# Second parts of the head stage's weights: made by an adding DMA instead of a vector difference

## The chip, the cores and the metric

The kernel runs on one core of a Trainium2 chip. The metric is the time of one execution on the device in microseconds (us). Three runs of the kernel before gave 1411.61, 1413.80 and 1413.81 us; the median is 1413.8 us. The profiled execution is a run of its own.

## The reference, cut to what matters

Two layers of a transformer trunk for 512 positions of width 1024, all in float32. Layer 0 mixes positions by an attention with 16 heads of 64 columns and a learned relative bias; layer 1 by a gated spatial mixing; each is followed by a squared-ReLU MLP. The change lies in layer 0's attention:

```python
q, k, v = jnp.split(h @ w_in, 3, axis=-1)
q = rms_norm(q.reshape(B, S, A_HEADS, A_HEAD_DIM), q_gain) * (A_HEAD_DIM ** -0.5)
k = rms_norm(k.reshape(B, S, A_HEADS, A_HEAD_DIM), k_gain)
...
s = jnp.einsum('bihd,bjhd->bhij', qc, kb).astype(jnp.float32) + bias
p = jax.nn.softmax(s, axis=-1).astype(vb.dtype)
return jnp.einsum('bhij,bjhd->bihd', p, vb)
...
return o @ w_out
```

`w_in` is 1024 x 3072 and `w_out` 1024 x 1024.

## The kernel before, in words

**Two parts of every operand.** TensorE multiplies in a rounded form of float32 (`float32r`). To keep the accuracy, each operand is held as a first part `hi` (the value rounded) and a second part `lo` (the value minus `hi`), and `mm3` adds up three products: hi x hi, hi x lo and lo x hi. Each weight tile is 128 x 1024 elements (512 KB). A DMA on SP's queue brings it from HBM into `raw`, ScalarE rounds it into `hi` (`A.copy`), VectorE subtracts (`V.tensor_tensor(lo, raw, hi)`), and `raw` goes back to the pool of 49 tiles (`SL`). A tile that is asked for waits until its last user is done with it.

**The stage.** Queries 0 to 11 and keys 0 to 7 are computed first. Then 16 heads run (`head_a` to `head_d`): transposes of queries and keys, a bias tile by DMA and a small memset of its corner on GpSimd, scores, softmax, transposes of the probabilities, the product with the values. In each pair of heads, GpSimd also spreads the reciprocals of the sums over a wide tile (the copy at L1210). Between the pieces of the heads, TensorE computes the rest of the projections: seven *fills* of 256 columns each (`filler`), in the order v0, v1, k2, q3, k3, v2, v3. Each fill multiplies four blocks of 128 rows by two weight tiles, here called a and b; the first multiplication of a block needs tile a's `hi`, the second its `lo`, and the thirteenth tile b. `fill_load` asks for the next fill's tiles while the one before is computed. `out_load(0)` and `out_load(1)` bring the two halves of `w_out`, four tiles each, called o0a to o0d and o1a to o1d; `out_early` multiplies the first three tiles of the first half while the last heads still run.

**What sets the order.** From the start of the heads to their end the order of instructions on every engine is set by a scheduler in the build, by its own estimate of durations; in the output projection behind them TensorE's order is the one written. On the chip each engine and each DMA queue runs its list strictly in order: whatever waits holds all that stands behind it. SP's queue issues all loads; GpSimd's (POOL's) list holds, in this stage, the sixteen memsets (L1178) and eight copies (L1210) alone.

Of the kernel before, what the change touches and what calls it, by code (L numbers as in the profile page):

```python
# [10 lines left out]
F32R = mybir.dt.float32r  # L11
I32 = mybir.dt.int32
AF = mybir.ActivationFunctionType
ALU = mybir.AluOpType
AX = mybir.AxisListType

P = 128
S = 512
D = 1024
NT = S // P  # L20
KD = D // P
# [31 lines left out]
def trunk_kernel(  # L53
# [20 lines left out]
    V, A, G, T, SP = nc.vector, nc.scalar, nc.gpsimd, nc.tensor, nc.sync  # L74
# [7 lines left out]
    SL = Slots(sp, NSLOT, "s")  # L82
    PS = Slots(pp, 8, "p")

    def f32(ap):
        return ap.bitcast(F32)
# [68 lines left out]
    def raw_tile(shape):  # L155

        t, i = SL.get(shape, F32)
        return t, lambda: SL.free(i)

    def flat(src, offset, ap):  # L160
        return bass.AP(tensor=src.tensor, offset=src.offset + offset, ap=ap)
# [217 lines left out]
    def wload(src, nk, k0=0, engs=(V,)):  # L379
        n = src.shape[1]  # L380
        kp = 1024 // n
        w, ids = [], []
        for k in range(k0, k0 + nk, kp):
            raw, done = raw_tile([P, kp, n])
            loaded[0] = SP.dma_start(raw, src[k * P:(k + kp) * P, :].rearrange("(k p) n -> p k n", p=P))
            hi, i = SL.get([P, kp, n], F32R)
            lo, j = SL.get([P, kp, n], F32R)
            A.copy(hi, raw)  # L388
            engs[len(ids) // 2 % len(engs)].tensor_tensor(lo, raw, f32(hi), ALU.subtract)  # L389
            done()  # L390
            w += [(hi[:, o, :], lo[:, o, :]) for o in range(kp)]
            ids += [i, j]
        return w, ids

    def wload_slabs(src, offset, count, n, engs=(V,)):

        w, ids = [], []
        for s in range(count):
            raw, done = raw_tile([P, 1024 // n, n])
            loaded[0] = SP.dma_start(  # L400
                raw.rearrange("p k n -> p (k n)"), flat(src, offset + s * P * 1024, [[1024, P], [1, 1024]])
            )
            hi, i = SL.get([P, 1024 // n, n], F32R)
            lo, j = SL.get([P, 1024 // n, n], F32R)
            A.copy(hi, raw)
            V.tensor_tensor(lo, raw, f32(hi), ALU.subtract)
            done()
            w += [(hi[:, o, :], lo[:, o, :]) for o in range(1024 // n)]
            ids += [i, j]
        return w, ids  # L410
# [111 lines left out]
    class Spent:  # L522
# [33 lines left out]
        def done(self, m):  # L556
            self.op.pop(m).free()
# [496 lines left out]
    for ci in range(1, 4):  # L1054
# [14 lines left out]
        k = ci * NC  # L1069
# [49 lines left out]
    with behind(), tc.issue_after(split[0].ins):  # L1119
        k_w, k_ids = wload_slabs(a_w_in, D * 768, 4, 512)  # L1120
# [167 lines left out]
    fw, fss, fps = {}, {}, [None]  # L1288

    def fill_load(n, cb):  # L1290
        if (n, cb) not in fw:
            i = {"q": -3, "k": -1, "v": 3}[n] + cb
            with tc.issue_after(split[0].ins), tc.issue_after(q_done.ins):
                fw[n, cb] = wload_slabs(a_w_in, D * (1280 + i * 256), 2, 256)

    def filler(count):
        for _ in range(count):
# [4 lines left out]
            if t == 0:  # L1302
                fill_load(n, cb)
                if (n, hf) not in qk:
                    qk_new(n, hf)
            if t == 2 and len(fill) > 2:
                fill_load(*fill[2][:2])
# [37 lines left out]
    out_w, out_ids, out_ps = {}, {}, {}  # L1345

    def out_load(hf):
        out_w[hf], out_ids[hf] = wload(a_w_out[0][:, hf * 512:hf * 512 + 512], KD)

    def out_early(t, n=6):  # L1350
        out_ps[t] = bank()
# [2 lines left out]
    for hd in range(H + 1):  # L1354
        if hd + 2 < H:
            head_a(hd + 2)
        filler(2 if hd < 10 else 1)
        bg(2 if hd < 8 else 1 if hd < 12 else 0)
        if hd + 1 < H:
            head_b(hd + 1)  # L1360
        if hd == 12:
            out_load(0)
        if H - 3 <= hd < H:
            out_early(hd - H + 3)
        if hd < H:
            head_c(hd)
        if hd > 0:
            head_d(hd - 1)
# [6 lines left out]
    in_order()  # L1375
    load_x()
    out_load(1)
    out_early(NT - 1)
    oTs = split_of(oT["t"])
# [102 lines left out]
    for hf in range(2):  # L1482
        raw, done = raw_tile([P, 4, P])
# [6 lines left out]
        a, i = SL.get([P, 2, 512], F32R)  # L1490
# [157 lines left out]
```

## Time and profile before

| what | value |
|---|---|
| median of three runs | 1413.8 us |
| profiled execution | 1417.19 us |
| its span, first to last instruction | 1415.2 us |
| TensorE busy, share of the span | 98% |
| VectorE busy, share of the span | 72% |
| ScalarE busy, share of the span | 50% |
| head stage | about 88 to 284 us of the span |

The profiled execution's span is 1.4 us above the median, so a difference that is worked out on the span is put onto the median. In the windows of the trace the columns are the length, the busy time of each engine (with its instructions), the granted clock of TensorE (1.00 is full speed), the busy share of the sixteen DMA engines and what they moved. In timelines a row has its start, its length, the engine and line, the operation, and in brackets how long the engine had stood idle before it and what ended that. "SPq" is the issue of a DMA on SP's queue; the load lands some microseconds later.

### The profile page before, as it was taken

Reading aid. Unit: us, or ns where it says so; the run is one execution under the profiler, and the core shown is the slowest. Engines: PE = TensorE matmul, PEld = TensorE weight load, DVE = VectorE, ACT = ScalarE, POOL = GpSimd, SP = SyncE. Lnnn points to the kernel's source line nnn. Section 1 sums busy time; section 2 is a strip of 40 time slices with the busy share of each in tenths; the row PEclk is TensorE's granted clock in tenths of the full one; section 3 lists DMA queues with packets and bytes.
Section 4 is the critical chain, followed back from the end, with each engine's and each line's share of the span. In section 5 each row is a group of like instructions: output and inputs, shape, how many; then the busy total and the mean of one; then the engine's idle time right before and its main releaser. Section 6 shows DMA issues by size and latency. Waiting matters only on the chain.

```text
span 1415.2 us, 18899 instructions
## 1 busy us (share of the span) xinstructions
PE 1390.1 (98%) x7226; PEld 1190.7 (84%) x7226; DVE 1021.7 (72%) x1494; ACT 710.7 (50%) x1229; POOL 9.5 (1%) x34
## 2 busy tenths in 40 slices
PE   9999988999999999999999998999999999999998
PEld 8899987789888888888888887888889988888887
DVE  6889998676668878777986745567577376866883
ACT  5537667555454544646677343134345355453630
POOL 0000000000000000000000000000000000000000
PEclk8999999999999999999999999999999999999999
DMA  9656566573253361456223344335437225242151
GB/s 371 241 141 212 168 182 189 177 278 106 77 193 120 121 221 60 147 181 223 82 82 120 134 134 141 96 106 186 131 114 276 75 79 189 60 149 89 30 164 60
DMA packets 82171, 208.94 MB, mean 148 GB/s; under 512 B 7576, under 2 KB 8992, under 8 KB 82080
## 3 DMA queue, kind: packets, MB, share of 16 engines
q1 hardware_dynamic: 82080, 207.72, 44.8%
q8 instruction: 57, 0.93, 0.3%
q14 instruction: 34, 0.28, 0.1%
HBM read 190.92 MB, written 8.39 MB: 141 GB/s over the span
## 4 chain that ended last, share of the span: by engine, by line
PE 88%; DMA 5%; DVE 3%; ACT 2%; SPq 1%; issue 1%; DVEq 0%; ACTq 0%
PE p L92 85%; DMA s<-in_a_w_in 2%; DMA s<-in_ada_w 1%; PE p L1546 1%; DMA s<-in_a_w_out 1%; PE p L1238 1%; PE p L315 1%; DMA s<-in_b_w_in 1%; SPq L1163 0%; DVE s L389 0%; ACT s L1205 0%; DVE s L955 0%; DMA s<-in_ffn_w 0%; DVE s L1200 0%; DVE s L1154 0%
## 5 line engine op out<-in xcount | busy, mean ns | idle before, releaser
L92 PE MATMUL p<-s,s 128*128 128x512 f32 (+2 forms) x6568 | 1325.6, 362 | 9.8 <-ACT s L388 2.8
L92 PEld LDWEIGHTS p<-s,s 128*128 128x128 f32 x6568 | 1112.8, 190 | 195.3 <-ACT s L388 3.2
L484 DVE TENSOR_TENSOR s<-s,s 128x1024 fp32r<-128x1024 f32 x234 | 280.2, 1220 | 108.0 <-PE p L92 52.8
L483 ACT CAST s<-s 128x1024 fp32r<-128x1024 f32 x234 | 241.7, 1051 | 173.7 <-PE p L92 108.2
L389 DVE TENSOR_TENSOR s<-s,s 128x1024 fp32r<-128x1024 f32 x80 | 96.4, 1219 | 59.0 <-ACT s L388 52.8
L388 ACT CAST s<-s 128x1024 fp32r<-128x1024 f32 x80 | 83.6, 1052 | 81.1 <-DMA s<-in_b_w_in 30.6
L631 DVE TENSOR_TENSOR s<-s,s 128x1024 f32<-128x1024 f32 x64 | 77.3, 1220 | 36.2 <-DMA s<-in_ffn_w 32.9
L739 ACT ACTIVATE r<-p 128x512 f32<-128x512 f32 x64 | 38.1, 595 | 114.8 <-PE p L92 114.8
L194 DVE SCALAR_TENSOR_TENSOR s<-s,cs,s 128x1024 f32<-128x1024 f32 x70 | 89.6, 1280 | 8.1 <-DMA s<-in_ada_w 7.3
L517 DVE TENSOR_TENSOR s<-p,s 128x512 f32<-128x512 f32 x104 | 70.4, 684 | 33.9 <-PE p L92 32.6
L745 ACT ACTIVATE s<-r 128x256 f32<-128x256 f32 (+1 forms) x112 | 44.9, 443 | 1.2
L424 DVE TENSOR_TENSOR tr<-p,s 128x512 f32<-128x512 f32 (+1 forms) x33 | 21.9, 669 | 30.3 <-PE p L92 30.1
L1205 ACT ACTIVATE s<-s,nm 128x128 f32<-128x128 f32 (+3 forms) x64 | 36.0, 564 | 6.8 <-DVE nm L1200 6.5
L1527 ACT CAST s<-s 128x512 fp32r<-128x512 f32 x24 | 14.5, 620 | 43.5 <-DVE s L1525 24.9
L1552 DVE TENSOR_TENSOR s<-p,s 128x256 fp32r<-128x256 f32 x48 | 19.9, 417 | 21.7 <-ACT s L1551 21.7
L1200 DVE CUSTOM_DVE_ANT_0 s<-p,s 128x128 f32<-128x128 f32 (+3 forms) x64 | 29.6, 484 | 7.8 <-issue 4.5
L1523 ACT ACTIVATE s<-p 128x512 f32<-128x512 f32 x24 | 14.4, 598 | 40.5 <-PE p L92 40.2
L530 DVE TENSOR_TENSOR s<-s,s 128x1024 f32<-128x1024 f32 x28 | 33.5, 1218 | 1.0 <-PE p L92 0.9
L304 ACT ACTIVATE s<-s 128x512 f32<-128x512 f32 x24 | 15.3, 637 | 34.0 <-DVE s L425 34.0
L1238 PE MATMUL p<-ident,s 128*128 128x128 f32 x160 | 25.2, 277 | 7.2 <-DVE s L1267 5.8
L1243 DVE TENSOR_TENSOR s<-p,s 128x512 fp32r<-128x512 f32 (+3 forms) x64 | 29.0, 483 | 3.8 <-ACT s L1242 3.4
L1242 ACT CAST s<-p 128x512 fp32r<-128x512 f32 (+3 forms) x64 | 25.0, 429 | 12.8 <-PE p L1238 12.5
(141 smaller groups left out, 760.6 us busy)
## 6 DMA issues: line engine op xcount, KB each, us to landing
s<-in_ffn_w SPq DMA_DIRECT2D x128, 512.0 KB, 4.6
s<-in_ada_w SPq DMA_DIRECT2D x96, 512.0 KB, 4.7
s<-in_b_w_in SPq DMA_DIRECT2D x48, 512.0 KB, 5.2
s<-in_b_w_out SPq DMA_DIRECT2D x24, 512.0 KB, 4.7
s<-in_a_w_in SPq DMA_DIRECT2D x22, 512.0 KB, 5.1
s<-s SPq DMA_DIRECT2D x64, 128.0 KB, 2.7
s<-in_x SPq DMA_DIRECT2D x8, 512.0 KB, 5.7
s<-in_a_rel_bias SPq DMA_DIRECT2D x16, 256.0 KB, 2.9
```

Source lines behind the costliest of these rows:

```text
L92: T.matmul(ps, lhsT, rhs, start=start, stop=stop, skip_group_check=more)
L194: V.scalar_tensor_tensor(acc, r, ck, acc, ALU.mult, ALU.add)
L388: A.copy(hi, raw)
L389: engs[len(ids) // 2 % len(engs)].tensor_tensor(lo, raw, f32(hi), ALU.subtract)
L483: A.copy(self.hi, raw)
L484: mark[0] = V.tensor_tensor(self.lo, raw, f32(self.hi), ALU.subtract)
L517: V.tensor_tensor(dst, ps, dst, ALU.add)
L631: V.tensor_tensor(x[0], y_[0], z[0], ALU.subtract)
L739: A.activation(r, ps, AF.Relu)
L745: A.activation(d, v, AF.Square)
L1205: A.activation(pt[it], pt[it], AF.Exp, bias=nm[:, it:it + 1], scale=-1.0, accum_out=sm[:, it:it + 1])
L1238: T.transpose(ps[:, it * P:(it + 1) * P], b["pt"][it][:, jt * P:(jt + 1) * P], ident)
```

## The change

A new function `wsplit` takes the place of `wload_slabs` for the seven fills (14 tiles) and of `wload` for the output weights (8 tiles). The load into `raw` and the rounding into `hi` stay. `raw` is given back as soon as it is rounded. Then ScalarE writes the negative of `hi` into `lo`, and a DMA that GpSimd issues reads the same weights from HBM a second time and adds them into `lo`. So each of 22 tiles loses one VectorE instruction, and gains one ScalarE instruction and one DMA of 512 KB on GpSimd's queue.

```diff
+    def wsplit(srcs, n):
+
+        w, ids = [], []
+        for src in srcs:
+            hi, i = SL.get([P, 1024 // n, n], F32R)
+            lo, j = SL.get([P, 1024 // n, n], F32R)
+            raw, done = raw_tile([P, 1024 // n, n])
+            SP.dma_start(raw, src)
+            A.copy(hi, raw)
+            done()
+            A.activation(lo, f32(hi), AF.Copy, scale=-1.0)
+            G.dma_start(lo, src, accum_op=ALU.add)
+            w += [(hi[:, o, :], lo[:, o, :]) for o in range(1024 // n)]
+            ids += [i, j]
+        return w, ids
...
             with tc.issue_after(split[0].ins), tc.issue_after(q_done.ins):
-                fw[n, cb] = wload_slabs(a_w_in, D * (1280 + i * 256), 2, 256)
+                fw[n, cb] = wsplit([
+                    flat(a_w_in, D * (1280 + i * 256) + s * P * 1024, [[1024, P], [256, 4], [1, 256]])
+                    for s in range(2)
+                ], 256)
...
     def out_load(hf):
-        out_w[hf], out_ids[hf] = wload(a_w_out[0][:, hf * 512:hf * 512 + 512], KD)
+        out_w[hf], out_ids[hf] = wsplit([
+            a_w_out[0][k * 256:k * 256 + 256, hf * 512:hf * 512 + 512].rearrange("(k p) n -> p k n", p=P)
+            for k in range(4)
+        ], 512)
```

The build's scheduler sets the head stage anew; behind it, from the end of the output projection's first multiplications on, TensorE's order is row for row the same. Line numbers of the changed kernel are higher by 16 to 22 from `gemm_tok` on. Three places of the order matter below.

**GpSimd's list around fills q3 and k3.** Before, between the copy of the second pair of heads and the copy of the fourth (L1210; the memsets at L1178 are those of heads 6 to 9):

```order
L1210 COPY s_153_1511<-rs 128x512
L1178 MEMSET s_178_1746 64x64
L1178 MEMSET s_186_1879 64x64
L1210 COPY s_182_1833<-rs 128x512
L1178 MEMSET s_205_2081 64x64
L1178 MEMSET s_215_2216 64x64
L1210 COPY s_209_2168<-rs 128x512
```

Now (L1226 are the copies, L1194 the memsets, L423 the adding DMAs; in the order of the list they are those of q3a, q3b, k3b, k3a and v2a):

```order
L1226 COPY s_153_1517<-rs 128x512
L423 DMA s_161_1569<-in_a_w_in 128x1024
L1194 MEMSET s_178_1754 64x64
L423 DMA s_164_1576<-in_a_w_in 128x1024
L1194 MEMSET s_186_1887 64x64
L1226 COPY s_182_1841<-rs 128x512
L423 DMA s_191_1898<-in_a_w_in 128x1024
L1194 MEMSET s_205_2091 64x64
L423 DMA s_188_1891<-in_a_w_in 128x1024
L1194 MEMSET s_215_2226 64x64
L423 DMA s_217_2230<-in_a_w_in 128x1024
```

The second tile of q3 stands behind the memset of head 6, both tiles of k3 behind the copy of the third pair, and k3a behind the memset of head 8 as well.

**GpSimd's list around the first half of the output weights.** Now (memsets of heads 13, 14 and 15, the copy of the seventh pair, and the adding DMAs of o0c, o0b, o0a and o0d):

```order
L1194 MEMSET s_270_2811 64x64
L1194 MEMSET s_281_2949 64x64
L423 DMA s_291_3018<-in_a_w_out 128x2x512
L1194 MEMSET s_299_3075 64x64
L1226 COPY s_283_3001<-rs 128x512
L423 DMA s_288_3011<-in_a_w_out 128x2x512
L423 DMA s_285_3004<-in_a_w_out 128x2x512
L423 DMA s_294_3025<-in_a_w_out 128x2x512
L1226 COPY s_307_3213<-rs 128x512
```

Tile o0a, which TensorE needs first, stands behind the memset of head 15, the copy of the seventh pair and o0b.

**SP's list around k3.** Before (L400 are the two loads of k3, L1163 the copies of keys between tiles, L1177 the bias tiles of heads 7 and 8):

```order
L1177 DMA s_186_1879<-in_a_rel_bias 128x512
L179 DMA s_179_1803<-in_ada_w 128x1024
L400 DMA s_187_1882<-in_a_w_in 128x1024
L1163 DMA s_175_1719<-s_177_1721 64x512 x4
L1163 DMA s_176_1720<-s_177_1721 64x512 x4
L400 DMA s_190_1888<-in_a_w_in 128x1024
```

Now:

```order
L1193 DMA s_186_1887<-in_a_rel_bias 128x512
L1179 DMA s_175_1727<-s_177_1729 64x512 x4
L1179 DMA s_176_1728<-s_177_1729 64x512 x4
L179 DMA s_193_1992<-in_ada_w 128x1024
L419 DMA s_192_1899<-in_a_w_in 128x1024
L419 DMA s_189_1892<-in_a_w_in 128x1024
```

Both loads of k3 now stand behind the eight key copies; before, k3a stood ahead of them.

## The prediction

> **What bounds the kernel now.** I read the page first. TensorE is the bound:
>
> ```profile
> span 1415.2 us, 18899 instructions
> PE 1390.1 (98%) x7226; PEld 1190.7 (84%) x7226; DVE 1021.7 (72%) x1494; ACT 710.7 (50%) x1229; POOL 9.5 (1%) x34
> ```
>
> All that TensorE stands idle in the whole span is 25 us. The order of its work differs only in the head stage, so I took that stage as one window:
>
> ```profile
> 88.00:284.00 196.00, 182.01 (x1276) 167.24 (x1275) 169.28 (x393) 128.76 (x300) 7.30 (x22) 0.97 0.61 184
> ```
>
> Here TensorE (first number after the length) is idle for 196.0 - 182.0 = 14.0 us, VectorE (third) is busy for 169 of 196 us, more than anywhere else, and the clock is 0.97, worth another 0.03 x 196 = 5.9 us. So **the whole gain that can be had is about 20 us**, however much VectorE is relieved. The timeline of TensorE shows where the idle time lies:
>
> ```profile
> 136.92 1.49 PE L92 MATMUL p<-s,s 128*128 128x512 f32 x8 [0.62 <-DVE nm L1200]
> 140.14 7.31 PE L92 MATMUL p<-s,s 128*128 128x256 f32 x56 [0.83 <-DVE nm L1200]
> 161.68 0.66 PE L1149 MATMUL p<-ident,s 128*128 128x128 f32 x4 [0.52 <-DVE nm L1200]
> 162.84 7.30 PE L92 MATMUL p<-s,s 128*128 128x256 f32 x56 [0.50 <-DVE nm L1200]
> 184.68 0.47 PE L92 MATMUL p<-s,s 128*128 128x256 f32 x2 [0.78 <-DVE s L1243]
> 186.90 5.24 PE L92 MATMUL p<-s,s 128*128 128x256 f32 x21 [1.75 <-ACT s L405]
> 241.38 0.83 PE L1238 MATMUL p<-ident,s 128*128 128x128 f32 x4 [3.12 <-DVE s L1267]
> 261.13 0.33 PE L1238 MATMUL p<-ident,s 128*128 128x128 f32 x1 [2.72 <-DVE s L1267]
> 262.07 5.98 PE L92 MATMUL p<-s,s 128*128 128x512 f32 x18 [0.61 <-DVE s L1243]
> ```
>
> Two kinds: small waits under 1 us on VectorE, and three of 1.75 to 3.3 us that stand beside weight tiles that came late (fill v2 at 186.90, o0 at 241, o1 at 261). After one of the second kind the clock is low for 5 us:
>
> ```profile
> 186.90:189.40 2.50, 2.50 (x7) 2.18 (x8) 2.50 (x9) 1.65 (x6) 0.00 (x0) 0.54 0.95 183
> 189.40:192.00 2.60, 2.60 (x16) 2.45 (x15) 2.60 (x11) 1.78 (x4) 0.00 (x0) 0.78 0.95 256
> ```
>
> That costs 0.46 x 2.5 + 0.22 x 2.6 = 1.7 us on top of the wait. I charge it to each new wait of 2 us or more.
>
> **The change part by part.** What leaves and what comes has its duration in the groups of this window:
>
> ```profile
> L406 DVE TENSOR_TENSOR s<-s,s 128x1024 fp32r<-128x1024 f32 x10 | 12.2, 1222 | 5.0 <-ACT s L405 4.7
> L405 ACT CAST s<-s 128x1024 fp32r<-128x1024 f32 x10 | 10.5, 1054 | 12.5 <-DMA s<-in_a_w_in 12.5
> L389 DVE TENSOR_TENSOR s<-s,s 128x1024 fp32r<-128x1024 f32 x8 | 9.7, 1217 | 2.8 <-ACT s L388 2.8
> ```
>
> VectorE loses 18 differences in the window, 12.2 + 9.7 = 21.9 us (four more, for v0 and v1, lie before it, under a TensorE that does not wait). ScalarE gains 18 negatives; for one I take the rounding of the same tile, 1.05 us, together 19 us onto 129 of 196: it stays below VectorE's load of before, so I cost it at nothing but latency. `raw` comes free one difference earlier, 1.2 us; nothing waits for it alone.
>
> What TensorE pays with is **latency of the second part**. Before, `lo` was there 1.22 us after `hi`. Now a negative and a DMA stand there. No adding DMA is in this trace. The nearest row is a plain load of the same 512 KB, issue to landing:
>
> ```profile
> L400 SPq DMA_DIRECT2D s<-in_a_w_in x18: 327/382/1105, 32.6 to 192.5; - x18
> DMA to landing us min/median/max: 3.6/5.0/9.3
> ```
>
> From below 3.6 us, the quickest. From above 10 us, two median loads one behind the other (read what stands there, then write the sum). An adding transfer has to read another 512 KB; the engines are busy at 0.61 in this window, so the added 11.5 MB find room. I take 6.0 us, near the plain median. The Trainium skill, "DMA: Bandwidth & Descriptors", section "Anatomy of one DMA — SWDGE (gpsimd) path", gives DMAs that GpSimd issues 2.0 us plus bytes / 436e3, an estimate of 3.2 us for this tile; by it the sum below falls under zero, and no row here shows such a DMA.
>
> Now each fill. The rows are the issue of its last load, the end of preparation before, GpSimd's items that the new DMAs stand behind, and TensorE's first use (quoted above for q3 at 140.14, k3 at 162.84, v2 near 186.9):
>
> ```profile
> 104.93 1.10 SPq L400 DMA_DIRECT2D s<-in_a_w_in  x1
> 111.50 1.21 DVE L406 TENSOR_TENSOR s<-s,s 128x1024 fp32r<-128x1024 f32 x1
> 118.12 7.28 PE L92 MATMUL p<-s,s 128*128 128x256 f32 x56
> 126.79 1.08 SPq L400 DMA_DIRECT2D s<-in_a_w_in  x2
> 131.61 2.58 DVE L406 TENSOR_TENSOR s<-s,s 128x1024 fp32r<-128x1024 f32 x2 [0.46 <-ACT s L405]
> 138.50 0.14 POOL L1178 MEMSET s<- 64x64 f32 x1 [8.56 <-PE p L92]
> 147.27 0.53 SPq L400 DMA_DIRECT2D s<-in_a_w_in  x1
> 154.65 1.22 DVE L406 TENSOR_TENSOR s<-s,s 128x1024 fp32r<-128x1024 f32 x1
> 157.28 0.61 POOL L1210 COPY s<-rs 128x512 f32<-128x512 f32 x1 [15.38 <-DVE ru L150]
> 159.83 0.14 POOL L1178 MEMSET s<- 64x64 f32 x1 [1.93 <-PE p L1238]
> 181.16 0.33 SPq L400 DMA_DIRECT2D s<-in_a_w_in  x1
> 188.21 1.22 DVE L406 TENSOR_TENSOR s<-s,s 128x1024 fp32r<-128x1024 f32 x1
> ...
> 179.40 0.53 SPq L179 DMA_DIRECT2D s<-in_ada_w  x1
> 201.45 1.22 DVE L406 TENSOR_TENSOR s<-s,s 128x1024 fp32r<-128x1024 f32 x1 [1.64 <-ACT s L405]
> 209.73 5.50 PE L92 MATMUL p<-s,s 128*128 128x256 f32 x43
> ```
>
> - *k2*: ready at 112.7 before, used from 118.4. Its second tile's DMA can start near 114 (load at 105, about 5 us to land, rounding, negative among ScalarE's other work) and lands at 120; TensorE comes to tile b after 12 multiplications of 0.13 us, at 120. **+0.3**.
> - *q3*: ready at 134.2. Tile a's DMA starts near 133 and is in time. Tile b's stands behind the memset of head 6, 138.50, which itself waits for a bias tile: lands at 138.7 + 6 = 144.7. TensorE wants b at 142.5 (12 multiplications and four score ones after 140.14, 2.3 us). **+2.2**, and its clock, **+1.7**.
> - *k3*: its DMAs stand behind the copy of 157.28, and tile a's behind the memset of 159.83 too: it lands at 166 and is wanted at 162.84. That is 3.2; but TensorE comes later by q3's wait, while only part of GpSimd's list moves with it. I take half, **+1.6**.
> - *v2*: the second load came at 181.16 and was ready at 189.43. Now it stands one load and one bias tile earlier on SP's list, at 179.40; with landing, rounding and negative the DMA starts at 186 and lands at 192. That is 2.6 later than before; half for the same reason, **+1.3**. Its clock is paid already.
> - *v0, v1, v3*: ready early enough; v3 had 7 us between 202.7 and 209.7, and its last load keeps its place on SP. **0**.
>
> For the output weights:
>
> ```profile
> 233.76 1.51 SPq L385 DMA_DIRECT2D s<-in_a_w_out  x3
> 240.73 0.61 POOL L1210 COPY s<-rs 128x512 f32<-128x512 f32 x1 [4.66 <-DVE rs L1206]
> 242.61 0.14 POOL L1178 MEMSET s<- 64x64 f32 x1 [1.27 <-DMA s<-in_a_rel_bias]
> 265.99 1.21 DVE L389 TENSOR_TENSOR s<-s,s 128x1024 fp32r<-128x1024 f32 x1
> 270.86 14.49 PE L92 MATMUL p<-s,s 128*128 128x512 f32 x65
> ```
>
> TensorE began with o0 right after 241.9. Now o0a stands behind the memset of head 15, the copy of the seventh pair and o0b: not before 242.6, landing at 248.6. The new order puts some 15 other instructions ahead, 2 us, so TensorE waits from 243.9. **+4.7**; the clock fell here before as well. o1 was ready at 267.2 and used 42 multiplications of 0.22 us after 270.86, at 280: its 13 us cover the DMAs. **0**; without that cover each microsecond would count in full.
>
> Sum of the costs: 0.3 + 2.2 + 1.7 + 1.6 + 1.3 + 4.7 = 11.8 us. What comes back: of 14.0 us idle, 1.75 and 3.12 are in my terms and 3.3 stands at the end (261 and 262), which leaves 5.8 us of small waits, nearly all on VectorE; 5 of them go. At the end VectorE stood behind a difference for o1; now ScalarE stands behind the rounding and a negative; I give back half of 3.3 + 1.7, 2.5 us. 11.8 - 7.5 = +4.3; I say **+5**, span 1420, and against the median of 1413.8 **1419 us**.
>
> **The rivals.**
>
> *Faster: the DMAs land fast.* With 3.6 us, q3 is in time, k3 waits 0.4, v2 nothing, o0 2.3, and no new clock loss: 2.7 against a relief of 7.5 to 10.8 (all small waits and the whole end). That is -5 to -8, **1407**. For it: VectorE is the fullest engine after TensorE, and the small waits are its. Against: the median row is 5.0, not 3.6, and the order on GpSimd's list delays the start whatever the landing. It decides below a landing of about 4.6 us. By the fit in the Trainium skill, "DMA: Bandwidth & Descriptors" (quoted above), this would be the case.
>
> *Much slower: an adding DMA takes two loads' time.* With 10 us: k2 4, q3 6, k3 7, v2 6, v3 3, o0 8.7 is 35; four more clock losses, 7; less 7.5: +34 at the most, and less where SP's loads move along with TensorE; I take +22, **1436**. For it: the DMA engines are over 0.9 busy around 187 (the clock rows above, 0.95), where every load waits. Against: 0.61 on average.
>
> *No difference.* Waits and relief cancel, within 0.2% (2.8 us, about what a measurement of this kernel can tell): **1414**. That the scheduler moved the loads early enough speaks for it; the rows of k2 and v3 do so.
>
> **How the numbers follow.** Slower by waits on second parts, 1417 to 1426: 0.42. Faster: 0.27. Slow DMAs: 0.17. No difference: 0.14. Faster by over 0.2% is the second, 0.27; the first loses a little at its lower edge to no change, so within 0.2% is 0.16 and slower 0.57. The range takes in most of the faster case and the slow one up to about 28 us: 1404 to 1440. The likeliest case alone spans 1415 to 1426.
>
> **What would show it.** In the changed profile VectorE falls by about 27 us (22 differences) and ScalarE rises by about 23. Issue to landing of GpSimd's DMAs decides: near 6 us for this forecast, under 4.6 for the faster rival, 10 for the slow one. TensorE's waits should be on the adding DMAs, at q3's and k3's second parts and longest at o0, while the waits on L1200 shrink. If TensorE's idle time in the stage is below 12 us, I am wrong; if the time moved outside the stage, the whole argument is.

## The result, and the profile after

The change makes the kernel **slower**: 1448.2 us median of five runs (1447.5 to 1449.8) against 1413.8 us (1411.6 to 1418.1) for the kernel before, a ratio of 1.0239 with a 95% interval of 1.0221 to 1.0257. That is +34 us where +5 was forecast, and outside the forecast range.

The page of the changed kernel, its head:

```profile
span 1447.1 us, 18979 instructions
PE 1396.9 (97%) x7226; PEld 1196.2 (83%) x7226; DVE 1001.7 (69%) x1472; ACT 731.4 (51%) x1251; POOL 32.8 (2%) x56
```

VectorE lost 20.0 us of work and ScalarE took on 20.7, as the change says. The span grew by 31.9 us. To see where, I cut both traces at landmarks that exist in both: the first key and query transposes of the heads (L1149 before, L1165 after) and the first transposes behind the output projection (L315). The window of the head stage so cut, first of the kernel before, then of the change (columns as in the prediction: length, busy time of TensorE, its weight loads, VectorE, ScalarE, GpSimd, then clock, busy share of the transfer engines, GB/s):

```profile
83.80:292.70 208.90, 194.91 (x1349) 178.43 (x1348) 178.31 (x409) 135.44 (x315) 7.30 (x22) 0.98 0.62 187
```

```profile
80.70:325.80 245.10, 205.99 (x1350) 188.44 (x1349) 162.16 (x391) 151.91 (x333) 26.95 (x40) 0.90 0.74 198
```

TensorE has the same matmuls in both; a few records are missing, so their counts differ by one. The stage is 36.2 us longer; of these, 25.1 us are idle time of TensorE (14.0 before, 39.1 now) and 11.1 us are the same matmuls running longer, under a clock of 0.90 instead of 0.98. Behind the stage nothing moved. The last 1131 us, first before, then after:

```profile
284.00:1415.00 1131.00, 1122.16 (x5492) 948.72 (x5491) 785.45 (x951) 537.82 (x852) 0.62 (x2) 1.00 0.40 132
```

```profile
316.00:1447.00 1131.00, 1122.84 (x5497) 949.26 (x5495) 785.47 (x951) 538.17 (x852) 0.61 (x2) 1.00 0.40 132
```

What TensorE waited for in the stage of the changed kernel (total us, times, longest):

```profile
PE p L92 <- DMA s<-in_a_w_in: 20.5, 5, 6.4
PE p L92 <- ACT s L1298: 6.9, 1, 6.9
...
PE p L1254 <- ACT s L1334: 2.6, 1, 2.6
```

The first row is 20.5 us that did not exist before. Its five waits stand in TensorE's timeline at second parts: those of tile b for k2, q3, v2 and v3, that of tile a for k3 (one multiplication of its first block had run). The two rows after them are the first half of the output weights, and the end of the stage:

```profile
120.95 7.53 PE L92 MATMUL p<-s,s 128*128 128x256 f32 x39 [3.54 <-DMA s<-in_a_w_in]
...
149.67 7.32 PE L92 MATMUL p<-s,s 128*128 128x256 f32 x40 [3.74 <-DMA s<-in_a_w_in]
...
177.65 8.75 PE L92 MATMUL p<-s,s 128*128 128x256 f32 x55 [6.42 <-DMA s<-in_a_w_in]
...
203.63 7.21 PE L92 MATMUL p<-s,s 128*128 128x256 f32 x43 [2.75 <-DMA s<-in_a_w_in]
...
230.32 1.43 PE L92 MATMUL p<-s,s 128*128 128x256 f32 x5 [4.08 <-DMA s<-in_a_w_in]
...
276.60 8.06 PE L92 MATMUL p<-s,s 128*128 128x512 f32 x34 [0.16 <-DMA s<-in_a_w_out]
...
309.96 8.24 PE L92 MATMUL p<-s,s 128*128 128x512 f32 x26 [6.85 <-ACT s L1298]
```

The adding DMA itself has a price now. Its line (the issue on GpSimd in ns, then the time from issue to landing in us):

```profile
L423 POOL DMA_DIRECT2D s<-in_a_w_in x14: 854/862/1027, 59.0 to 219.7; - x14
L423 POOL DMA_DIRECT2D s<-in_a_w_out x8: 1188/1196/1210, 256.0 to 294.8; - x8
...
DMA to landing us min/median/max: 5.6/7.6/11.1
```

A median of 7.6 us where 6.0 were assumed. The pieces of the chain of waits that end in the five waits above (start, length; the one of ScalarE is the negative that k3's DMA waited for) are these:

```profile
112.25 8.65 DMA s<-in_a_w_in
...
142.44 7.20 DMA s<-in_a_w_in
...
168.70 0.97 ACT s L422
169.96 7.65 DMA s<-in_a_w_in
...
196.47 7.12 DMA s<-in_a_w_in
...
219.73 10.55 DMA s<-in_a_w_in
```

The transfer engines (the sixteen DMA engines) are now busier. The queues between 88 and 300 us of the changed kernel (packets, MB, share of the 16 engines' time):

```profile
q1 hardware_dynamic: 13696, 32.51, 51.0%
q0 software_dynamic: 3449, 9.13, 25.0%
```

SP's transfers take 0.510 x 212 / 32.51 = 3.3 us of the sixteen engines for each MB; the adding ones take 0.250 x 212 / 9.13 = 5.8 us.

The wait at the end has another cause. ScalarE's list has three roundings of the next weights (L499) ahead of the last heads' product (L1298):

```profile
298.96 1.05 ACT L499 CAST s<-s 128x1024 fp32r<-128x1024 f32 x1 [2.86 <-DMA s<-in_ffn_w]
303.17 1.04 ACT L499 CAST s<-s 128x1024 fp32r<-128x1024 f32 x1 [3.16 <-DMA s<-in_ffn_w]
...
308.35 1.04 ACT L499 CAST s<-s 128x1024 fp32r<-128x1024 f32 x1 [3.53 <-DMA s<-in_ffn_w]
309.30 0.61 ACT L1298 CAST s<-s 128x512 fp32r<-128x512 f32 x1
```

and SP could issue the loads for those only behind the second half of the output weights, which waited for tiles:

```profile
274.15 11.93 SPq L419 DMA_DIRECT2D s<-in_a_w_out  x4
293.34 2.76 SPq L728 DMA_DIRECT2D s<-in_ffn_w  x2
```

The third of these loads, issued at 301.30, waited besides for a difference on VectorE that ran at 300.04: that of the first of these weights, whose `raw` tile it needed.

### The profile page after: what moved, and what is told of

It reads as the page before. It is cut to its first block, busy times and chain, and to the rows that moved or that the text cites. A ratio compares the mean times of both kernels' runs of the same rounds, so it can differ in the third digit from the quotient of the medians.

```text
span 1447.1 us, 18979 instructions
## 1 busy us (share of the span) xinstructions
PE 1396.9 (97%) x7226; PEld 1196.2 (83%) x7226; DVE 1001.7 (69%) x1472; ACT 731.4 (51%) x1251; POOL 32.8 (2%) x56
## 4 chain that ended last, share of the span: by engine, by line
PE 84%; DMA 8%; ACT 3%; DVE 3%; issue 1%; SPq 0%; POOL 0%; DVEq 0%; ACTq 0%; POOLq 0%
PE p L92 81%; DMA s<-in_a_w_in 4%; DMA s<-in_a_w_out 2%; DMA s<-in_ffn_w 1%; DVE s L971 1%; ACT s L420 1%; PE p L1568 1%; DMA s<-in_ada_w 1%; PE p L315 1%; DMA s<-in_b_w_in 0%; ACT s L422 0%; PE p L1254 0%; DVE s L389 0%; ACT s L1221 0%; SPq L1179 0%
## 5 line engine op out<-in xcount | busy, mean ns | idle before, releaser
L92 PE MATMUL p<-s,s 128*128 128x512 f32 (+2 forms) x6568 | 1335.7, 364 | 38.8 <-DMA s<-in_a_w_in 20.5
L500 DVE TENSOR_TENSOR s<-s,s 128x1024 fp32r<-128x1024 f32 x234 | 280.7, 1221 | 114.0 <-PE p L92 56.3
L499 ACT CAST s<-s 128x1024 fp32r<-128x1024 f32 x234 | 241.5, 1051 | 178.3 <-PE p L92 107.5
L389 DVE TENSOR_TENSOR s<-s,s 128x1024 fp32r<-128x1024 f32 x72 | 86.8, 1221 | 55.6 <-ACT s L388 48.8
L388 ACT CAST s<-s 128x1024 fp32r<-128x1024 f32 x72 | 75.2, 1052 | 76.8 <-DMA s<-in_b_w_in 23.2
L1259 DVE TENSOR_TENSOR s<-p,s 128x256 fp32r<-128x256 f32 (+3 forms) x64 | 29.2, 484 | 19.4 <-ACT s L1258 19.1
L1549 ACT CAST s<-s 128x512 fp32r<-128x512 f32 x24 | 14.5, 620 | 43.7 <-DVE s L1547 25.1
L420 ACT CAST s<-s 128x1024 fp32r<-128x1024 f32 x22 | 22.9, 1045 | 15.8 <-DMA s<-in_a_w_out 11.1
```

Source lines behind the costliest of these rows:

```text
L92: T.matmul(ps, lhsT, rhs, start=start, stop=stop, skip_group_check=more)
L499: A.copy(self.hi, raw)
L500: mark[0] = V.tensor_tensor(self.lo, raw, f32(self.hi), ALU.subtract)
```

## The experiments

The runs of the kernel before that stood beside these had medians of 1413.9 to 1415.8 us. Ratios are to those beside them. "Stage" is the window between the two landmarks above, in the one profiled execution of each kernel; TensorE has 1349 or 1350 matmuls in it in all of them, and it leaves out what the first 90 us did in that execution. One execution is not the median: the profiled ones of "only output weights", "all, plain write" and "differences on GpSimd" were 6.2 to 7.4 us below the medians of their kernels, that of the control further down 4.7 us above. So the medians carry the comparisons, and the stages say where to look.

### Which half, and which property of the DMA

Three kernels: only the fills changed; only the output weights changed; and all changed, but the second transfer overwrites instead of adding.

```diff
 e1_fills: the output weights as before
-        out_w[hf], out_ids[hf] = wsplit([...], 512)
+        out_w[hf], out_ids[hf] = wload(a_w_out[0][:, hf * 512:hf * 512 + 512], KD)

 e2_out: the fills as before
-                fw[n, cb] = wsplit([...], 256)
+                fw[n, cb] = wload_slabs(a_w_in, D * (1280 + i * 256), 2, 256)

 e3_plain: in wsplit
-            G.dma_start(lo, src, accum_op=ALU.add)
+            G.dma_start(lo, src)
```

> Only the seven fills take the adding DMA; the output weights keep VectorE's difference. Theory (TensorE waits in order for second parts that land 7.5 us after the DMA's issue, and its clock falls behind each wait): the fill half of the stage grew from 126 to 148 us in the changed kernel, so about +22 us, 1436 us, with TensorE's waits on the adding DMAs again near 20 us. Rival (the loss comes from the end of the stage, where ScalarE's list holds TensorE up): no more than +8 us, 1422 us.

> Only the output weights take the adding DMA; the fills keep the difference. Theory: the output half of the stage grew from 70 to 80 us, so about +10 us, 1424 us, the sum with the other half near the whole +34. Rival (the two halves share one cause, a stage that is full of transfers): less than +4 us, because without the fills' DMAs the transfers find room, and the sum of both halves is well below 34.

> The changed kernel with GpSimd's DMA as a plain write in place of an adding one: same place, same size, but the second part then holds the whole weights and not the difference (that part of the computation is left out). Theory A (adding is what makes the DMA slow, because it reads the old contents too): issue to landing falls from 7.6 us to the 5 us of a plain load, TensorE's waits lose about 2.5 us each, and the time falls by 12 to 18 us, to 1430 to 1436. Theory B (the path over GpSimd and the busy transfer engines make it slow, adding costs nothing): landing stays above 7 us and the time within 4 us of 1448.

| kernel | median us | ratio [95%] | stage us | clock there |
|---|---|---|---|---|
| only fills | 1437.0 | 1.0162 [1.0139, 1.0186] | 232.0 | 0.93 |
| only output weights | 1431.2 | 1.0123 [1.0099, 1.0146] | 220.5 | 0.94 |
| all, plain write | 1425.8 | 1.0076 [1.0051, 1.0101] | 214.9 | 0.97 |

The fills alone cost 23 us and have the same waits as the change:

```profile
PE p L92 <- DMA s<-in_a_w_in: 20.4, 5, 7.6
```

The output weights alone cost 17, where about 10 were expected, so the halves add up to 40, more than the 34 of both. Each kernel has an order of its own; that this makes the difference is not shown.

The plain write is the cleanest comparison of the study, since its order is row for row that of the changed kernel on every engine. What it leaves out is the sum: the second part then holds the whole weights. **It is 22 us faster than the change** (1448.2 - 1425.8), where 12 to 18 were expected. Its line and its wait:

```profile
L423 POOL DMA_DIRECT2D s<-in_a_w_in x14: 528/528/731, 59.2 to 203.2; - x14
L423 POOL DMA_DIRECT2D s<-in_a_w_out x8: 696/705/715, 233.2 to 268.2; - x8
...
DMA to landing us min/median/max: 4.0/5.0/8.9
...
PE p L92 <- DMA s<-in_a_w_in: 6.0, 4, 3.4
```

It is issued in 0.53 and 0.70 us instead of 0.86 and 1.20 and lands at 5.0 instead of 7.6 us; TensorE's waits for second parts fall from 20.5 to 6.0 us. So two thirds of the loss are the adding, not the second transfer, the negative or the new order.

### Is it TensorE's waiting alone?

In the next kernel VectorE makes `lo` as before, and the negative and the adding DMA go to a tile of the pool that nobody reads. A companion with the same order on TensorE, VectorE, ScalarE and SP writes plainly; a third one has the negative, but no second DMA.

```diff
 e4_shadow, in wsplit (e7_shadow_plain: without accum_op; e9_shadow_no_dma: without the DMA)
+            V.tensor_tensor(lo, raw, f32(hi), ALU.subtract)
             done()
-            A.activation(lo, f32(hi), AF.Copy, scale=-1.0)
-            G.dma_start(lo, src, accum_op=ALU.add)
+            idle, ii = SL.get([P, 1024 // n, n], F32R)
+            A.activation(idle, f32(hi), AF.Copy, scale=-1.0)
+            G.dma_start(idle, src, accum_op=ALU.add)
+            SL.free(ii)
```

> VectorE makes the second parts as before, and ScalarE's negative and the adding DMA are carried out beside it on a tile that nobody reads. Theory (TensorE's waiting for the second part is the cause): all the added work of ScalarE, GpSimd and the transfer engines stays, but TensorE waits no longer for it, so the time lies near the kernel before, 1414 to 1424. Rival (the added transfers and instructions themselves slow everything else in the stage): 1435 or more.

> The run in which the added work is done on a tile that nobody reads, with GpSimd's DMA as a plain write in place of an adding one. Every list stands as in that run (1449 us); only the DMA's kind differs, and TensorE never waits for it. If the adding DMA hurts by what it does to the other transfers and to the tiles it holds, the time falls by 12 us or more, to 1437 or less, as it did where TensorE waited (1448 to 1426). If it hurts only because TensorE waits for its result, nothing changes: 1445 to 1452, and that run's loss lies in the work of ScalarE and VectorE.

> The same with no second DMA at all: VectorE makes the second parts, ScalarE writes 22 negatives that nobody reads. It prices ScalarE's added 23 us and the extra tile. If these make the loss of that run (1449 us), the time stays above 1435. If the second transfer does, it lies at 1414 to 1422.

| kernel | median us | ratio [95%] | stage us |
|---|---|---|---|
| adding, unread | 1449.5 | 1.0241 [1.0214, 1.0269] | 241.5 |
| plain, unread | 1433.9 | 1.0138 [1.0119, 1.0156] | 230.2 |
| no second DMA | 1420.0 | 1.0041 [1.0027, 1.0056] | 213.9 |

My theory at that point, that the loss is TensorE's waiting for second parts, **fell**: nobody reads the result, and the kernel is as slow as the change. The line of that DMA shows who waited for it instead:

```profile
  ACT s L1261: 8.6, 3
  DVE s L1219: 5.9, 1
  ACT s L1177: 4.5, 1
  ACT s L502: 3.8, 2
...
DMA to landing us min/median/max: 5.5/7.3/10.9
```

The tile goes back to the pool only when the DMA has landed, and the next user of that tile, with all that stands behind it on ScalarE and VectorE, waits. So this experiment did not take the dependency away, it moved it. It did show that adding costs 15.6 us more than writing here too, at one order. The plain writes in their turn cost 13.9 us against the kernel without the second DMA. How much of that is the transfer, how much the tile it holds and how much the other order is not separated.

### Earlier loads

If the wait for second parts is a matter of a few us, asking for the fills' weights two blocks earlier should take it away.

```diff
 e5_early: the changed kernel, e6_before_early: the kernel before
-            if t == 2 and len(fill) > 2:
-                fill_load(*fill[2][:2])
+            if t == 0 and len(fill) > 3:
+                fill_load(*fill[3][:2])
```

> The changed kernel, with each fill's weights asked for two of its four blocks earlier (when the fill before starts, not when it is half done). Theory (TensorE waits for second parts that come 3 to 7 us too late): half a fill is 7 to 10 us, more than any wait of the fills, so their 20 us of waits mostly go and the time falls to 1420 to 1432; the output weights' part stays. Rival (the added transfers slow the stage whoever waits): the time stays within 5 us of 1448, the waits appear elsewhere.

> The kernel before with the same earlier loads of the fills, as the measure for the run with earlier loads in the changed kernel. Both theories: its fills were ready 6 us before their use except one, so no more than 3 us either way, 1411 to 1417, unless the tiles held longer delay other loads.

The changed kernel went from 1448.2 to 1437.9 us (ratio 1.0160 [1.0140, 1.0179], stage 231.3); the kernel before went to 1420.0 (1.0031 [1.0013, 1.0049], stage 214.2). The waits of TensorE on the fills are gone from the trace of the former, and others have come:

```profile
PE p L92 <- DMA s<-in_a_w_out: 7.0, 1, 7.0
PE p L92 <- DMA s<-s: 6.5, 5, 3.3
```

The first is o0, the second are the copies of keys between tiles, which stand on SP's list among the loads. So 20.5 us of direct waits bring back 10 us when they go, and between the two early kernels 18 us remain. The time lies between what the two theories expected (1420 to 1432, or within 5 us of 1448), and the early kernel before is 3 us above what both expected.

### What the relief of VectorE is worth

The kernel before, with the fills' differences on GpSimd: VectorE is relieved of 14 of the 22 and no transfer is added.

```diff
 e8_pool_diff: in wload_slabs of the kernel before
-            V.tensor_tensor(lo, raw, f32(hi), ALU.subtract)
+            (G if n == 256 else V).tensor_tensor(lo, raw, f32(hi), ALU.subtract)
```

> The kernel before with the differences of the fills' weights (14 of 128 x 1024) made by GpSimd instead of VectorE: VectorE is relieved as by the change, of 14 of the 22, and no transfer is added. GpSimd's copy of 128 x 512 took 0.67 us in the kernel before, so a difference of 128 x 1024 is estimated at 1.3 to 3 us against 1.1 on VectorE. The prediction's own term, a relief of 7.5 us from fewer waits on VectorE: 1406 to 1411. Rival 'VectorE was never the limit there': within 3 us of the kernel before, 1411 to 1417. Slower than 1420 would mean that the latency of the second part decides even at a few us.

1424.3 us, ratio 1.0064 [1.0040, 1.0088], stage 215.4: slower than before, and 4 us above the 1420 beyond which the expectation would have the latency decide. A difference takes 2.48 us on GpSimd, 1.22 on VectorE:

```profile
L406 POOL TENSOR_TENSOR s<-s,s 128x1024 fp32r<-128x1024 f32 x10 | 24.8, 2481 | 31.1 <-ACT s L405 24.2 <-ACT s L1205 6.0 <-PE p L92 0.9
```

No gain showed from this relief, at least not at 1.3 us more latency.

### Does a second transfer cost anything if nobody waits?

A first pair added a transfer of half the bytes to the kernel before, into a tile that I took to be private; in truth another load of SP's list writes it later.

```diff
 f_add, f_plain (without accum_op): behind each rounding of those weights in the kernel before
+            G.dma_start(beside, src, accum_op=ALU.add)     # half of the tile, 256 KB
```

> The kernel before, with one transfer more behind every rounding of a fill's or the output's weights: a plain write, issued by GpSimd, of half of the weights just loaded (256 KB of 512) into one tile of its own that nothing reads. The arithmetic stays that of the kernel before; 22 transfers, 5.8 MB, half of what the change added. Nobody waits for them and no tile of the shared pool is held by them. Theory 'the transfer engines are shared': the earlier pair gave +14 us for 11.5 MB of plain writes, so half of that, +7, 1421 to 1422. Rival 'only waiting and held tiles cost': nothing here waits, so within 3 us of the kernel before, 1412 to 1417.

> The same as the plain one of this pair, with the same order on every engine, but the transfer adds to the tile. Theory 'the transfer engines are shared, and adding occupies them 1.74 times as long': half of the +15.6 us measured between the earlier adding and plain pair, so +8 over the plain one, 1429 to 1430. Rival 'only waiting and held tiles cost': within 3 us of the plain one.

1432.2 us (1.0129 [1.0109, 1.0150]) and 1444.3 us (1.0214 [1.0192, 1.0236]), far more than either theory expected, and not for its question: the transfers did not stay behind their roundings but ran one after the other from 2 us on, and the load of `gain` had to wait for the last of them (issued at 132.84 us in the plain kernel, at 145.77 in the adding one). SP's wait at that load, of the plain, then of the adding kernel (total us, times, longest):

```profile
SPq L1514 <- DMA beside<-in_a_w_out: 6.4, 1, 6.4
```

```profile
SPq L1514 <- DMA beside<-in_a_w_out: 17.1, 1, 17.1
```

The fill's weights stand right behind that load on SP's list and wait with it. The pair says nothing about the transfer engines; it shows what one load that must wait costs on a list that is worked off in order.

The second pair moves the rounded tile, all 512 KB of it, to places in the chip's memory that nothing else uses, behind a rounding by a real dependency; the control has only the four transfers at the start that fill those places.

```diff
 g_add, g_plain (without accum_op), g_none (without this line): behind each rounding of those weights
+            G.dma_start(beside[sent[0] % 4], hi.bitcast(F32).rearrange('p a b -> p (a b)'), accum_op=ALU.add)
```

> The kernel before with four transfers more at its very start (512 KB each, from the input into four places of the chip's memory that nothing reads), as the control of the two that follow. Both theories: within 4 us of the kernel before, 1412 to 1419.

> The control, and behind the rounding of each of the 22 tiles of fill and output weights a plain transfer of the rounded tile, 512 KB, by GpSimd, into those four places. The arithmetic is that of the kernel before; nobody reads what is written, and the tile that is read stays in use longer anyway. 11.5 MB as in the change. Theory 'the transfer engines are shared': about the +14 us that plain transfers cost in the earlier pair, 1427 to 1434. Rival 'only waiting and held tiles cost': within 4 us of the control.

> The same as the plain one with the same order of instructions, but each transfer adds to what it finds. Theory 'the transfer engines are shared, and adding occupies them longer' (5.8 us against 3.35 us of the sixteen engines for each MB): 10 to 18 us over the plain one, 1437 to 1450. Rival 'only waiting and held tiles cost': within 4 us of the plain one.

| kernel | median us | ratio [95%] | stage us | first transposes at us |
|---|---|---|---|---|
| none (control) | 1428.9 | 1.0099 [1.0079, 1.0120] | 217.2 | 93.2 |
| plain | 1423.8 | 1.0064 [1.0047, 1.0081] | 215.3 | 86.2 |
| adding | 1436.2 | 1.0147 [1.0123, 1.0171] | 221.4 | 92.4 |

The windows of the stage, of the plain and then of the adding kernel:

```profile
86.20:301.50 215.30, 198.92 (x1349) 183.11 (x1347) 177.67 (x410) 135.52 (x315) 17.01 (x40) 0.95 0.72 225
```

```profile
92.40:313.80 221.40, 197.22 (x1349) 181.75 (x1347) 178.66 (x410) 135.50 (x315) 22.48 (x40) 0.95 0.81 219
```

**The plain transfers showed no cost**: with the engines at 0.72 instead of 0.60 the stage is 1.9 us shorter than the control's and the whole 5.1 us shorter, so my theory that sharing the engines costs some 14 us fell for plain transfers. The control has another order in the stage, so a cost of a few us is not excluded. The adding ones, at the same order as the plain ones, cost 12.4 us; in the profiled executions 6.1 us of the difference lie in the stage and 6.2 ahead of the first transposes. The latter were there already at 40 us, when none of the transfers had run (the first is issued at 60.7 us in the plain kernel, at 66.9 in the adding one). The first 40 us, of the plain and then of the adding kernel:

```profile
0.00:40.00 40.00, 31.75 (x181) 26.79 (x182) 24.26 (x55) 21.45 (x38) 3.46 (x12) 1.00 0.97 372
```

```profile
0.00:40.00 40.00, 32.36 (x142) 27.76 (x143) 18.82 (x45) 17.19 (x32) 3.51 (x12) 0.79 0.97 370
```

So in this pair of executions 6 us stand where the adding transfers ran. Whether the six runs of each kernel, whose medians differ by 12.4, started as differently as these two is not on record: the price of adding with nobody behind it lies between 6 and 12 us, and where is left open.

The control missed its own expectation: it is 13.5 us slower than the kernel before, and its profiled execution is 9.4 us longer ahead of the stage and 8.3 in it. The four transfers at the start alone do not set the former, since the plain kernel has them too and was only 2.4 us later. Every kernel here whose stage the scheduler set anew, with no second transfer in it or with one that hardly anybody waits for, has a stage of 213.9 to 217.2 us against 208.9: earlier loads 214.2, no second DMA 213.9, differences on GpSimd 215.4, control 217.2, plain write 214.9. The medians of the first three are 5.1, 5.1 and 8.5 us above the kernel before. So 5 to 8 us of the change's loss may be the order alone. That is argued from neighbours; an order of the changed kernel that equals the old one was not tried.

No kernel of the study is faster than the kernel before.

## Why the prediction was wrong

The side was right, and so was the place: all of the loss lies in the head stage. The mechanism was right in part. TensorE's longest waits on the fills are on second parts, as forecast, and taking the adding out brings back 22 of the 34 us. But with the fills' waits gone (earlier loads) only 10 came back, and adding cost 15.6 us where nobody reads its result: it also holds up other loads and tiles, for which the prediction had no term. The size was wrong: +34 for +5. Against its own sum of +4.3, the stage shows +36.2, and the difference splits into three terms. This is bookkeeping of one trace, not an experiment.

**Waits, +17.5.** Forecast 10.1 without the clock, measured 20.5 + 0.2 + 6.9 = 27.6.
- *The failed step is "I take 6.0 us" for the adding DMA.* The five pieces of the chain quoted above are 8.65, 7.20, 7.65, 7.12 and 10.55 us long, 41.2 in all. Where each was wanted follows from the timeline (its end less the wait): 5.2, 3.5, 1.3, 4.4 and 6.5 us behind the issue, 20.8 in all (for k3: 177.65 - 6.42 - 169.96 = 1.3). The forecast had nearly these leads (6, 3.8 and 2.8 for k2, q3 and k3). With 6.0 us each the waits would have been 0.8 + 2.5 + 4.7 + 1.6 = 9.7 us instead of 20.5 (v3 in time); the size of the landing explains 10.8 of the 17.5. A check: with 5.0 us each the same leads give 0 + 1.5 + 3.7 + 0.6 + 0 = 5.8 us, and the plain write, which lands at a median of 5.0, had 6.0. The bounds of 3.6 and 10 us held the medians, and the choice near the plain load's 5.0 was the wrong end: an adding DMA occupied the engines 1.7 times as long for each byte (5.8 against 3.35 us for each MB).
- *"I take half", for k3 and v2, failed too.* The reason given was that only a part of GpSimd's list moves with TensorE, so that a wait pays for some of the next. Tile a of k3 was forecast to land at 166; it was only issued at 169.96, right behind ScalarE's negative of 168.70. TensorE wanted it 8.4 us later than forecast (171.2 for 162.84), and the issue came 10 us later than the 160 it was forecast at. The lists that feed the DMAs moved with TensorE, by at least as much. This and the smaller differences of the leads account for 9.7 - 5.4 = 4.3 us; 5.4 is the forecast for the four fills.
- *o0 was forecast at 4.7 and took 0.2; o1 at 0, and the end took 6.9*, 2.4 more in sum. No wait on o1's own DMAs stands in the trace, so the 13 us of multiplications did cover them. What was not followed was what waits behind the load of o1 on SP and behind the next weights on ScalarE.

**Clock, +9.4.** One loss of 1.7 us was charged. The same matmuls took 11.1 us longer. Where there had been three waits of 1.75 to 3.12 us there are seven of 2.6 to 6.85. Behind k3's wait the clock was this:

```profile
177.65:180.15 2.50, 2.50 (x11) 2.50 (x12) 2.20 (x10) 0.24 (x1) 0.00 (x0) 0.50 1.04 245
180.15:182.75 2.60, 2.60 (x20) 2.60 (x19) 1.40 (x3) 0.00 (x0) 0.00 (x0) 0.79 0.53 151
```

That is 0.50 x 2.5 + 0.21 x 2.6 = 1.8 us. Such windows behind all seven waits show a clock of 0.50 to 0.80 and add up to 15.5 us, those behind the three waits before to 5.1: 10.4 us more, near the measured 11.1. So the price of one wait was about right, 2.2 us for 1.7; the number of waits was not. The prediction charged it at q3 alone, since it had the other waits under 2 us or where the clock had fallen before.

**Relief, 5.0 less than thought.** Idle time other than the waits above fell from 14.0 to 39.1 - 27.6 = 11.5 us, 2.5 instead of 7.5. The kernels without second transfers but with less VectorE work or earlier loads did not gain either.

17.5 + 9.4 + 5.0 = 31.9, and 4.3 + 31.9 = 36.2. Ahead of the stage the profiled execution was 3.1 us quicker and behind it 1.2, which leaves the 31.9 us of the span.

"The engines are busy at 0.61 in this window, so the added 11.5 MB find room" did not hold for an adding transfer. SP's own loads show it: the 512 KB weights at L179 went from a median landing of 4.5 to 5.6 us, the 256 KB bias tiles from 2.8 to 4.8. With plain writes at the same order, the engines at 0.74, they were at 4.9 and 4.0, so part of this comes with any second transfer. The rows of 88 to 284 us, of before and then of after (operations, KB each, median landing):

```profile
s<-in_ada_w SPq DMA_DIRECT2D x17, 512.0 KB, 4.5
...
s<-in_a_rel_bias SPq DMA_DIRECT2D x13, 256.0 KB, 2.8
```

```profile
s<-in_ada_w SPq DMA_DIRECT2D x16, 512.0 KB, 5.6
...
s<-in_a_rel_bias SPq DMA_DIRECT2D x13, 256.0 KB, 4.8
```

Of the rivals, the slow one ("an adding DMA takes two loads' time", at most +34) was nearest, with a landing of 7.6 rather than 10 us but none of the discount. It got 0.17. That its +34 is also the measured one is luck: it had 35 us of waits, 8.7 of them at o0, where 27.6 came, and it gave back 7.5 us where 2.5 came. The faster one needed a landing under 4.6 us; the quickest adding DMA of 512 KB in any run landed at 5.3. The Trainium skill, "DMA: Bandwidth & Descriptors", section "Anatomy of one DMA — SWDGE (gpsimd) path", would give 3.2 us for this tile (an estimate from its fit); the traces disagree for this loaded stage, with 5.0 us for the plain and 7.6 us for the adding transfer by GpSimd.

The signs named ahead were there: VectorE fell (20 us instead of 27), ScalarE rose by 20.7, the waits stand on the adding DMAs of q3 and k3, nothing moved outside the stage. The longest wait on a second part was k3's, not o0's.

What stays open: of the 12 us by which the plain write is still slower than the kernel before, how much is its 6 us of waits, how much the second transfer and how much the order. Open too is how the 22 us of the adding divide between waits on its results and what it does to the other transfers.

## What to carry to other kernels

A DMA that adds is not a plain load with a small surcharge: here, at 512 KB, it took 1.4 to 1.5 times the landing and 1.7 to 2.2 times the engines' time of a plain one. Count the landing in full wherever the result is wanted a few us after its issue. Before an operation is moved from a busy engine to a DMA, look up by how much the result was early: 1.2 us on an engine that was 0.85 busy was cheaper than 7.6 us on engines that were 0.6 busy. And an estimate for a stage whose order is set anew needs a term for that order: here every kernel with a new order and no such DMAs had a stage 5 to 8 us longer, at 209 before; that the order alone did it is not shown.

## What the hardware showed that was not expected

- Adding against plain, 512 KB by GpSimd at one and the same order: landing 7.6 against 5.0 us, time of the sixteen engines 5.8 us (above) against 0.149 x 212 / 9.44 = 3.35 us for each MB, and issue on GpSimd 0.86 against 0.53 us (fills) and 1.20 against 0.70 us (output weights). The other two pairs of 512 KB landed at 7.3 against 5.1 us (unread tile) and 7.8 against 5.7 us (to the chip's memory); in the last one the engines' time was 0.248 x 212 / 9.44 = 5.6 against 0.113 x 212 / 9.44 = 2.5 us for each MB. The queue's row of the plain kernel, 88 to 300 us:

```profile
q0 software_dynamic: 3616, 9.44, 14.9%
```

- 11.5 MB more by plain transfers in a stage whose engines were 0.60 busy cost no time that could be told from the control, whose order is another.
- Behind the seven waits of 2.6 to 6.85 us TensorE's clock was 0.50 to 0.80 over the next 2.5 us, and 0.50 to 0.79 over the 2.6 us behind those.
- A difference of 128 x 1024 took 2.48 us on GpSimd, twice VectorE's 1.22.
